# FFN 1's second matrix: hidden tiles 2 and 3 as a sixth half-size group of the seven-product scheme, and a new order of work around the transposes behind it

## The chip, the cores and the metric

The kernel runs on one core of a Trainium2 chip. The metric is the time of one execution on the device in microseconds; the number that counts is the median of several runs. The engines are TensorE (PE; PEld is its weight load), VectorE (DVE), ScalarE (ACT), GpSimd (POOL) and SyncE (SP, which here only starts transfers). POOL starts the transfers that add into SBUF.

## What is computed

One layer of a streaming encoder on 512 tokens of width 1024, all in float32: half-step FFN 1, a mixer (recurrent branch and attention) and half-step FFN 2, each between RMS norms. What matters here is FFN 1 and the entry of the mixer:

```python
f = swiglu(rms_norm(h, ffn1_pre_g), ffn1_w1, ffn1_w3, ffn1_w2)   # (silu(x @ w1) * (x @ w3)) @ w2, hidden width 2816
h = h + 0.5 * rms_norm(f, ffn1_post_g)
u = rms_norm(h, mix_pre_g)
... = u @ w_in                                                   # xr is its first part here
```

## The kernel before, in words

**Split numbers.** Every float32 operand of a matmul is split into a high part (a copy in a format that TensorE takes at full rate) and a low part (the difference). `split2` (L224) does it: ScalarE writes the copy (L226), VectorE the difference (L227). A product is then three matmuls: high x high, high x low, low x high.

**FFN 1's first matrices.** The hidden width has 22 tiles of 128. Tiles 0 to 3 (`NC1 = 4`) are computed one by one. Tiles 0 and 1 (`NG = 2`) go through silu at once; of tiles 2 and 3 the two products are copied to the buffers `kept`, and gate (`gate_kept`, L1357), silu (`silu_kept`, L1360) and product (`swiglu_kept`, L1363) come later, at hooks of the next stage (`KEPT_AT`). Tiles 4 to 21 come in pairs (`Pairs`, L844): each of 18 jobs makes one product of two tiles from seven smaller ones and prepares the weights of the next job meanwhile (`prep`). The dictionary `late` hangs further work on points (job, place) of these pairs.

**FFN 1's second matrix** (`w2a`; helpers `blocks` L759, `Halves` L601, `tok_gemm` L378). `GS_A` lists groups of hidden tiles: (4, 6) stands for tiles 4, 5, 6, 7, and there are five such groups, `G = 5`, 20 tiles. Each group's product with the matrix, cut in two halves of hidden tiles, tokens and columns, is made with seven products instead of eight. They are named, in the order of the work, m1, m5, m2, m6, m3, m7, m4 (L607). Product m of group i is **unit** number u = (place of m) x G + i; within a name the groups add into the same PSUM banks: m1, m6, m7 and m4 into `bu`, m5 and m3 into `bx`, m2 into `bc`, each a pair of banks for two token tiles. A unit of two tile pairs is 12 matmuls of 512 columns (`unit`, L716): 2 pairs, 2 token tiles, 3 matmuls. A group with one entry in its tuple has one pair of tiles and half of everything: 6 matmuls, operands of half width, high and low of the weights in one buffer.

Each unit needs operands, and `prep` (L686) makes them in unit order: one split of a weight tile, one split of a hidden tile, and the sums for later products (`sums`, L662). The second and further weight operands come by transfers that add into a negated copy (`T`, L647: ScalarE negates, POOL starts the transfer); `t1` and `s1` do the first of these ahead of time, from the pairs' points. `step(u)` (L749) prepares up to unit u + 4 (`LEAD = 5`), runs the **hooks** of u, issues the unit's matmuls and, behind the last group of m1, m5, m6 and m7, has the banks copied or added out (`out`, L732).

**Tiles 2 and 3** (`TAIL_A`) are no group. They are multiplied the plain way (`classical`, L426, through `mm_tok`, L249 to L257): 4 token tiles x 2 column halves x 2 hidden tiles x 3 matmuls of 512 columns. Their weights are loaded and split by `tails` (L421), their hidden tiles by `Hidden.to` (L590) into `hT`.

**From FFN 1 to the mixer** (`tok_gemm`, L434 to L482, and L501 to L555). With token tiles t = 0 to 3 the written order is: units of m1 to m3; plain products of t = 0 and 1; two more preps; the first of the mixer's weights `xr` split (`x_split`); norm(0); the units of m7; plain products of t = 2, 3 (one half); preps of m4; norm(1); the units of m4 for their first token tile, `step(u, (0,))`; transposes tr(0) of the normed tile of t = 0; a plain product; the first unit of m4 for its second token tile; tr(1); norm(2); the other units of m4; a last plain product; the mixer's first `xr` unit for tokens 0 to 255 (`start`, L504, 24 matmuls of 256 columns); tr(2); norm(3); two more such units; tr(3); a fourth; then tokens 256 to 511 of all four.

`norms` (L326) is two norms in a row (the FFN's post norm and the mixer's pre norm) on ScalarE and VectorE; it writes `hg`, half by VectorE (L345), half by ScalarE (L346), stores the new residual by SP (L342), and calls `mid` in its middle. Where a part of the sum was copied out before, the norm begins with an add (L308). `transpose_mm` (L349) turns `hg` on TensorE into `tr`, `transpose_out` (L359) splits it into `uT`, the operand of the mixer, and `transpose_xf` (L371) copies it for later sums.

Each engine does its instructions in the order in which the program writes them, and so does each queue of transfers (SP's, POOL's). Buffers come from one pool of 42 slots of 4 KB per partition and from 8 PSUM banks; an instruction that reuses one waits for the last reader. `MARKS_A` and `X_AT` give the steps at whose hooks the tail's loads, the residual's loads (`h_back`) and the `xr` loads are started. FFN 2's second matrix (`w2b`, `last_gemm`, L797) has six groups already, `GS_B`, the last of them `(20,)`, of half size, and no plain tiles; no mixer follows it.

Of the kernel before, what the change touches and what calls it, by code (L numbers as in the profile page):

```python
# [13 lines left out]
ALU = mybir.AluOpType  # L14
# [37 lines left out]
def hybrid_layer(ctx: ExitStack, tc: tile.TileContext, a: dict, out: bass.AP):  # L52
# [14 lines left out]
    def bank(name="ps"):  # L67
        uid[0] += 1
        return pp.tile([P, 512], F32, tag="ps", name=f"{name}_{uid[0]}")
# [308 lines left out]
    def tok_gemm(nm, xs, n, R, gpost_name, scale, gpre_name, first, x_to=None, xf=None, spill=False, then=None, eps=None, pre=None):  # L378
# [5 lines left out]
        acc = {}  # L384
# [36 lines left out]
        def tails():  # L421
            for i, k in enumerate(tail):
                x_to(F + i + 1)
                w[k] = get(nm, k, ahead=max(0, len(tail) - 1 - i), rawahead=0 if pre else 2)

        def classical(t, n_):  # L426
            for k in tail:
                new = k == tail[0] and (t > 1 and n_ == 1 if pre else k == 0)
                mm_tok(accs(t), xs[k], t, w[k], new, k == tail[-1], (n_,), bool(pre))

        def norm(t, mid=None):
            us[t] = norms(acc[t], t, g[0], scale, g[1], spill, ep(t), mid, pre and pre.part(t), (1, 0) if pre and t > 1 else (0, 1))

        if pre:  # L434
            G = pre.G
            pre.hooks[3 * G].append(vectors)
            pre.hooks[4 * G + 2].append(lambda: act.activation(small(1, "tiny"), veps[:, 0:1], AF.Abs_reciprocal_sqrt))
            pre.hooks[4 * G].append(lambda: act.activation(g[1], g[1], AF.Copy, scale=NEWT))
            x0 = st["get"] + len(tail)
            for i, u in enumerate(X_AT):  # L440
                pre.hooks[u].append(lambda i=i: dma_to(x0 + i + 1))

            def x_split(i, parts=(0, 1)):
                for p in parts:
                    dma_split(x0 + i, p)

            for u in range(5 * G):
                pre.step(u)
            tails()
            for t in range(2):  # L450
                acc[t] = [pre.bank["bc"][t], pre.bank["bx"][t]]
                for n_ in range(2):
                    classical(t, n_)
            pre.prep(5 * G + LEAD + 2)
            x_split(0)
            norm(0, lambda: x_split(1))
            pre.cap = 7 * G - 2
            for u in range(5 * G, 6 * G):
                pre.step(u)
            pre.cap = 7 * G  # L460
            for t in range(2, 4):
                acc[t] = [pre.bank["bu"][t - 2], bank("acc")]
                classical(t, 1)
            pre.prep(7 * G)
            pre.hid.eo.clear()
            x_split(2)
            norm(1, lambda: x_split(3, (0,)))
            for u in range(6 * G, 7 * G):
                pre.step(u, (0,))
            trs[0] = transpose_mm(us[0])  # L470
            transpose_out(trs[0], 0)
            classical(2, 0)
            pre.step(6 * G, (1,))
            trs[1] = transpose_mm(us[1])
            transpose_out(trs[1], 1)
            transpose_xf(trs[0], 0, xf)
            norm(2, lambda: [x_split(3, (1,)), transpose_xf(trs[1], 1, xf, (0,))])
            transpose_xf(trs[1], 1, xf, (1,))
            for u in range(6 * G + 1, 7 * G):
                pre.step(u, (1,))  # L480
            classical(3, 0)
            pre.bank.clear()  # L482
        else:
            tails()
            vectors()
            split_to(st["get"] + len(first))
            dma_to(st["split"] + 2)
            for t in range(NT):
                for n_ in range(2):
                    classical(t, n_)  # L490
                if t == NT - 1:
                    break
                if t >= 1:
                    trs[t - 1] = transpose_mm(us[t - 1])
                if t == NT - 2:
                    transpose_out(trs[t - 1], t - 1)
                norm(t)
                if t == 1:
                    transpose_out(trs[t - 1], t - 1, xf)
# [16 lines left out]
        k0, k1 = range(KT // 2), range(KT // 2, KT)  # L516
        if pre:
            start()
            trs[t - 1] = transpose_mm(us[t - 1])
            norm(t, between)  # L520
            transpose_out(trs[t - 1], t - 1, parts=(1,))
            start()
            start()
        else:
            start(range(3))
            trs[t - 1] = transpose_mm(us[t - 1])
            mm_feat(bs[0], ws[0], 0, 256, ks=range(3, KT))
            norm(t, between)
            transpose_out(trs[t - 1], t - 1, parts=(1,))
            transpose_xf(trs[t - 2], t - 2, xf, (1,))  # L530
            start()
            start(range(1))
# [5 lines left out]
            then()  # L538
        if not pre:
            mm_feat(bs[2], ws[2], 0, 256, ks=k0[1:])  # L540
        start()
        get_ahead()
        mm_feat(bs[0], ws[0], 256, 512)
        mm_feat(bs[1], ws[1], 256, 512)
# [214 lines left out]
    def blocks(nm, hid, pairs, late, h_src, gs, marks, in_slots, loads):  # L759
# [19 lines left out]
        if pairs.R is None:  # L779
            late[end - 4, 1] = [lambda i=i: half.s1(i) for i in range(4)]  # L780
            late[end - 3, 1] = [lambda: half.load(3)]
            late[end - 2, 1] = [lambda i=i: half.t1(i) for i in range(2)]
            late[end - 1, 2] = [lambda: half.prep(1, False)]
            late[end, 1] = [lambda: half.t1(2)]
        else:
            late[5, 1].append(lambda: half.s1(0))
            late[9, 1].append(lambda: half.s1(1))
            late[13, 1] = [lambda: half.s1(2)]
            for i in (1, 2, 3):
                late.setdefault((end, i), []).insert(0, lambda i=i: half.t1(i - 1))  # L790
            late[end, 1].append(lambda: half.s1(3))
            for i in (3, 4):
                hooks[i - 3].append(lambda i=i: half.t1(i))
        pairs.run(ahead, late)
        return half
# [566 lines left out]

    def swiglu_kept(f):  # L1363
        t = kept.pop(f)
        dve.tensor_tensor(out=t[:, 1, :], in0=t[:, 0, :], in1=t[:, 1, :], op=ALU.mult)
        hid.f[f] = t[:, 1, :]

    X1.update((b, uview(*q)) for b, q in (("b11", (0, 0)), ("b21", (1, 0)), ("b22", (1, 1))))
    P_ = pairs_a.prep
# [23 lines left out]
    late[4, 2], late[5, 2] = [softplus_exp], [softplus_ratio]  # L1393
    late[5, 3], late[6, 2] = [lambda: softplus_terms((13, 11, 9))], [lambda: softplus_terms((7, 5))]
    late[7, 2], late[8, 2] = [lambda: softplus_terms((3, 1))], [softplus_out]

    h.clear()
    half = blocks("w2a", hid, pairs_a, late, lambda t: a["x"][t * P : (t + 1) * P, :], GS_A, MARKS_A, 6 * len(GS_A), LOAD_A)
    X1 = pairs_a = late = None
    for fn, at_ in zip((gate_kept, silu_kept, swiglu_kept), KEPT_AT):  # L1400
        for f, u in zip(range(NG, NC1), at_):
            half.hooks[u].insert(0, lambda f=f, fn=fn: fn(f))
    xf = {(hh, th): slot([P, 4, 256], name="xf") for hh in range(2) for th in range(2)}
    bs = tok_gemm(
        "w2a", hid, FT, len(TAIL_A), "ffn1_post_g", 0.5, "mix_pre_g", [("xr", i) for i in range(4)], xf=xf, spill=True, eps=veps, pre=half)
# [446 lines left out]

BY_POOL = {("wg", i) for i in range(2, 8)} | {("wk", 0), ("wk", 1)}

TAIL_A = (2, 3)
KEPT_AT = (15, 16), (18, 19), (19, 20)
LEAD = 5
U_SLOTS = 4
LOAD_A, LOAD_B = (0, 3, 5, 5), (0, 4, 5, 6)
GS_A = (4, 6), (8, 10), (12, 14), (16, 18), (0, 20)  # L1860
MARKS_A = (17, 18), (21, 22), (23, 26, 28, 29)
X_AT = (22, 24, 26, 28)

TAIL_B = ()
GS_B = (0, 2), (4, 6), (8, 10), (12, 14), (16, 18), (20,)
# [6 lines left out]
NC1 = 4  # L1872
# [57 lines left out]
```

## Time and profile before

| | us |
|---|---|
| median of 3 runs | 1100.61 (1100.34 to 1101.22) |
| the profiled execution | 1100.36 |
| its span, first to last instruction | 1098.4 |
| TensorE busy, share of the span | 1089.5, 99% |
| VectorE busy | 930.2, 85% |
| ScalarE busy | 707.6, 64% |
| POOL busy | 418.0, 38% |

A row of a timeline has the start in us, the duration in us, the engine, the line of the kernel, the operation, what it writes and reads, the shape, and how many are merged; a bracket at its end is the idle time of the engine before it and what ended it. `whi` and `wlo` are the split weights, `hx` and `uT` the split hidden tiles of a unit. A row of groups has, behind the bar, busy time and mean duration in ns of one. A row of waits has engine, tile and line of who waited, for whom, the sum in us, how often, and the longest. A row of windows has the stretch, its length, busy time of PE, PEld, DVE, ACT and POOL with the number of instructions, TensorE's granted clock, the share of the DMA engines and GB/s. A matmul's duration is longer than the distance from one to the next, since they overlap.

### The profile page before, as it was taken

To read this page: it belongs to the slowest core of one execution; us is meant where nothing else is said; L and a number is where in the kernel's file an instruction comes from. 1 tells how busy PE (TensorE), PEld (TensorE's weight loads), DVE (VectorE), ACT (ScalarE), POOL (GpSimd) and SP (SyncE) were. 2 spreads that over 40 slices of the span, in tenths; PEclk is the share of its full clock that TensorE was granted. 3 is DMA by queue.
4 is the path that set the end of the run, shared out by engine and by line. 5 is a ranking of instruction groups with operands and counts; after the bars stand their busy time and mean duration, and the time that the engine had idled before them with its cause. 6 is when DMAs were issued, how large, how long until landed. Compare 5 with 4: busy or idle time off the path is not lost.

```text
span 1098.4 us, 18110 instructions
## 1 busy us (share of the span) xinstructions
PE 1089.5 (99%) x6856; PEld 986.2 (90%) x6856; DVE 930.2 (85%) x1334; ACT 707.6 (64%) x1230; POOL 418.0 (38%) x348
## 2 busy tenths in 40 slices
PE   9999999999999999999999999999999999999997
PEld 8899999998888878899888888888999999998886
DVE  5987999989988998887778867767889989889996
ACT  7756555598878778656656654446555455578872
POOL 0144933232002513242556573010877656633200
PEclk9999999999999999999999999999999999999999
DMA  9325663389767642156122335352323323449923
GB/s 340 120 83 143 131 150 115 105 187 231 218 171 228 178 122 77 39 173 249 58 95 79 114 136 211 137 188 85 129 78 115 108 86 108 147 101 239 213 75 134
DMA packets 53895, 156.46 MB, mean 142 GB/s; under 512 B 5536, under 2 KB 7456, under 8 KB 53808
## 3 DMA queue, kind: packets, MB, share of 16 engines
q1 hardware_dynamic: 40848, 124.59, 32.3%
q0 software_dynamic: 12672, 30.19, 14.8%
q8 instruction: 54, 0.88, 0.3%
q10 hardware_dynamic: 288, 0.52, 0.1%
q14 instruction: 33, 0.27, 0.1%
HBM read 139.57 MB, written 13.62 MB: 139 GB/s over the span
## 4 chain that ended last, share of the span: by engine, by line
PE 93%; DVE 3%; ACT 2%; DMA 1%; issue 1%; DVEq 0%; POOL 0%; ACTq 0%; POOLq 0%
PE c L838 13%; PE c L839 13%; PE c L840 13%; PE f L237 9%; PE f L238 9%; PE f L239 9%; PE hw L728 5%; PE hw L729 5%; PE hw L730 5%; PE acc L257 1%; PE acc L256 1%; PE acc L255 1%; PE pt L1692 1%; DMA raw_xr<-in_xr_dram 1%; DVE wlo L227 1%
## 5 line engine op out<-in xcount | busy, mean ns | idle before, releaser
L839 PE MATMUL c<-uT,wlo 128*128 128x256 f32 x516 | 146.0, 283 | 0.0
L840 PE MATMUL c<-uT,whi 128*128 128x256 f32 x516 | 146.0, 283 | 0.0
L838 PE MATMUL c<-uT,whi 128*128 128x256 f32 x516 | 146.0, 283 | 0.0
L838 PE MATMUL c<-Xh,whi 128*128 128x256 f32 x504 | 142.7, 283 | 0.0
L839 PE MATMUL c<-Xh,wlo 128*128 128x256 f32 x504 | 142.6, 283 | 0.0
L237 PE MATMUL f<-uT,whi 128*128 128x512 f32 (+1 forms) x380 | 138.6, 365 | 0.0
L238 PE MATMUL f<-uT,wlo 128*128 128x512 f32 (+1 forms) x380 | 136.9, 360 | 0.0
L239 PE MATMUL f<-uT,whi 128*128 128x512 f32 (+1 forms) x380 | 136.9, 360 | 0.0
L840 PE MATMUL c<-Xl,whi 128*128 128x256 f32 x456 | 129.0, 283 | 0.0
L227 DVE TENSOR_TENSOR wlo<-S,whi 128x1024 fp32r<-128x1024 f32 x86 | 121.0, 1407 | 5.9 <-POOL OL L1728 3.1
L226 ACT ACTIVATE whi<-S 128x1024 fp32r<-128x1024 f32 x86 | 88.5, 1054 | 29.1 <-DVE S L887 28.0
L839 PEld LDWEIGHTS c<-uT,wlo 128*128 128x128 f32 x516 | 99.0, 192 | 0.2
L838 PEld LDWEIGHTS c<-uT,whi 128*128 128x128 f32 x516 | 99.0, 192 | 0.2
L840 PEld LDWEIGHTS c<-uT,whi 128*128 128x128 f32 x516 | 99.0, 192 | 0.0
L838 PEld LDWEIGHTS c<-Xh,whi 128*128 128x128 f32 x504 | 96.8, 192 | 0.3 <-issue 0.3
L839 PEld LDWEIGHTS c<-Xh,wlo 128*128 128x128 f32 x504 | 96.8, 192 | 0.0
L728 PE MATMUL hw<-whi,uT 128*128 128x512 f32 x228 | 88.7, 389 | 0.0
L730 PE MATMUL hw<-whi,uT 128*128 128x512 f32 x228 | 88.7, 389 | 0.0
L840 PEld LDWEIGHTS c<-Xl,whi 128*128 128x128 f32 x456 | 87.5, 192 | 0.0
L729 PE MATMUL hw<-wlo,uT 128*128 128x512 f32 x216 | 84.0, 389 | 0.0
L237 PEld LDWEIGHTS f<-uT,whi 128*128 128x128 f32 x380 | 71.7, 189 | 12.1 <-issue 1.7
L239 PEld LDWEIGHTS f<-uT,whi 128*128 128x128 f32 x380 | 71.7, 189 | 10.9
(435 smaller groups left out, 3209.8 us busy)
## 6 DMA issues: line engine op xcount, KB each, us to landing
raw_w1b<-in_w1b_dram SPq DMA_DIRECT2D x22, 512.0 KB, 4.2
raw_w3b<-in_w3b_dram SPq DMA_DIRECT2D x22, 512.0 KB, 4.4
raw_w3a<-in_w3a_dram SPq DMA_DIRECT2D x21, 512.0 KB, 5.0
raw_w1a<-in_w1a_dram SPq DMA_DIRECT2D x20, 512.0 KB, 4.4
raw_w2a<-in_w2a_dram SPq DMA_DIRECT2D x17, 512.0 KB, 5.4
raw_wg<-in_wg_dram SPq DMA_DIRECT2D x16, 512.0 KB, 3.5
raw_w2a<-in_w2a_dram POOLq DMA_DIRECT2D x15, 512.0 KB, 9.4
raw_w2b<-in_w2b_dram SPq DMA_DIRECT2D x15, 512.0 KB, 6.3
```

What stands on the lines that cost most here:

```text
L226: act.activation(hi, src, AF.Copy)
L227: dve.tensor_tensor(out=lo, in0=src, in1=f32(hi), op=ALU.subtract)
L237: pe.matmul(ps[:, c0:c1], wh[:, s], h_, start=k == 0 and c0 == 0, stop=False, skip_group_check=True)
L238: pe.matmul(ps[:, c0:c1], wl[:, s], h_, start=False, stop=False, skip_group_check=True)
L239: pe.matmul(ps[:, c0:c1], wh[:, s], l_, start=False, stop=k == KT - 1, skip_group_check=True)
L255: pe.matmul(acc[n], x[:, 0, c], wh[:, s], start=first, stop=False, skip_group_check=skip)
L728: pe.matmul(ps, xs[:, 0, j, c], hi[:, j, :], start=start and j == 0, stop=False, skip_group_check=True)
L729: pe.matmul(ps, xs[:, 0, j, c], lo[:, j, :], start=False, stop=False, skip_group_check=True)
L730: pe.matmul(ps, xs[:, 1, j, c], hi[:, j, :], start=False, stop=i == self.G - 1, skip_group_check=True)
L838: pe.matmul(ps, wh[:, s], xh, start=first, stop=False, skip_group_check=True)
L839: pe.matmul(ps, wl[:, s], xh, start=False, stop=False, skip_group_check=True)
L840: pe.matmul(ps, wh[:, s], xl, start=False, stop=k == 3, skip_group_check=True)
```

## The change

Tiles 2 and 3 become a sixth group `(2,)` of half size, so `G` is 6 and there are 42 units, u0 to u41, with the half-size ones at u5, u11, u17, u23, u29, u35 and u41. `TAIL_A` is empty; the plain products, their loads and their splits are gone. Gate, silu and product of tiles 2 and 3 move from hooks of this stage to jobs 1 and 2 of the pairs, and the product is written to the group's buffer. The early negations (`t1`) start one place earlier. The preps are cut anew around norm(0), the last two units of m7 are run one token tile after the other, and two units of m4 instead of one stand between tr(0) and tr(1). Behind it the mixer's second `xr` unit is cut in two halves of 12 matmuls, one ahead of tr(2), one behind it, and the fourth likewise around tr(3). The hooks' step numbers are moved to suit.

```diff
             for u in range(5 * G):
                 pre.step(u)
-            tails()
             for t in range(2):
                 acc[t] = [pre.bank["bc"][t], pre.bank["bx"][t]]
-                for n_ in range(2):
-                    classical(t, n_)
-            pre.prep(5 * G + LEAD + 2)
+            pre.prep(5 * G + LEAD + 3)
             x_split(0)
             norm(0, lambda: x_split(1))
-            pre.cap = 7 * G - 2
-            for u in range(5 * G, 6 * G):
+            pre.prep(7 * G - 2)
+            for u in range(5 * G, 6 * G - 2):
                 pre.step(u)
-            pre.cap = 7 * G
+            for t in range(2):
+                for u in range(6 * G - 2, 6 * G):
+                    pre.step(u, (t,))
+                if t == 0:
+                    pre.prep(7 * G)
             for t in range(2, 4):
-                acc[t] = [pre.bank["bu"][t - 2], bank("acc")]
-                classical(t, 1)
-            pre.prep(7 * G)
+                acc[t] = [pre.bank["bu"][t - 2], None]
             pre.hid.eo.clear()
             x_split(2)
             norm(1, lambda: x_split(3, (0,)))
...
             trs[0] = transpose_mm(us[0])
             transpose_out(trs[0], 0)
-            classical(2, 0)
-            pre.step(6 * G, (1,))
+            for u in range(6 * G, 6 * G + 2):
+                pre.step(u, (1,))
             trs[1] = transpose_mm(us[1])
             transpose_out(trs[1], 1)
-            transpose_xf(trs[0], 0, xf)
-            norm(2, lambda: [x_split(3, (1,)), transpose_xf(trs[1], 1, xf, (0,))])
+            x_split(3, (1,))
+            norm(2, lambda: [transpose_xf(trs[0], 0, xf), transpose_xf(trs[1], 1, xf, (0,))])
             transpose_xf(trs[1], 1, xf, (1,))
-            for u in range(6 * G + 1, 7 * G):
+            for u in range(6 * G + 2, 7 * G):
                 pre.step(u, (1,))
-            classical(3, 0)
...
         if pre:
             start()
+            start(k0)
             trs[t - 1] = transpose_mm(us[t - 1])
             norm(t, between)
             transpose_out(trs[t - 1], t - 1, parts=(1,))
+            mm_feat(bs[1], ws[1], 0, 256, ks=k1)
             start()
-            start()
+            start(k0)
...
-        start()
+            start()
+        else:
+            mm_feat(bs[3], ws[3], 0, 256, ks=k1)
...
+            late[11, 2] = [lambda: half.s1(5)]
             late[13, 1] = [lambda: half.s1(2)]
-            for i in (1, 2, 3):
-                late.setdefault((end, i), []).insert(0, lambda i=i: half.t1(i - 1))
+            for at_, i in (((end - 1, 3), 0), ((end, 1), 1), ((end, 2), 2)):
+                late.setdefault(at_, []).insert(0, lambda i=i: half.t1(i))
             late[end, 1].append(lambda: half.s1(3))
-            for i in (3, 4):
+            for i in (3, 4, 5):
                 hooks[i - 3].append(lambda i=i: half.t1(i))
...
-        dve.tensor_tensor(out=t[:, 1, :], in0=t[:, 0, :], in1=t[:, 1, :], op=ALU.mult)
-        hid.f[f] = t[:, 1, :]
+        hid.f[f] = hid.place(f)
+        dve.tensor_tensor(out=hid.f[f], in0=t[:, 0, :], in1=t[:, 1, :], op=ALU.mult)
...
+    for at_, fn in zip(((1, 2), (2, 1), (2, 2)), (gate_kept, silu_kept, swiglu_kept)):
+        late[at_] = [lambda f=f, fn=fn: fn(f) for f in range(NG, NC1)]
...
-    for fn, at_ in zip((gate_kept, silu_kept, swiglu_kept), KEPT_AT):
-        for f, u in zip(range(NG, NC1), at_):
-            half.hooks[u].insert(0, lambda f=f, fn=fn: fn(f))
...
-TAIL_A = (2, 3)
-KEPT_AT = (15, 16), (18, 19), (19, 20)
+TAIL_A = ()
...
-GS_A = (4, 6), (8, 10), (12, 14), (16, 18), (0, 20)
-MARKS_A = (17, 18), (21, 22), (23, 26, 28, 29)
-X_AT = (22, 24, 26, 28)
+GS_A = (4, 6), (8, 10), (12, 14), (16, 18), (0, 20), (2,)
+MARKS_A = (), (), (27, 31, 33, 34)
+X_AT = (26, 28, 31, 33)
```

## The prediction

> **What bounds the kernel now.** I read the page's first lines, then the view of waits for TensorE alone, then the timeline of TensorE over the stage that the change touches.
>
> ```profile
> span 1098.4 us, 18110 instructions
> PE 1089.5 (99%) x6856; PEld 986.2 (90%) x6856; DVE 930.2 (85%) x1334; ACT 707.6 (64%) x1230; POOL 418.0 (38%) x348
> PE tr L355 <- DVE hg L345: 0.8, 2, 0.6
> ```
>
> TensorE is the bound of the whole kernel: after its start it waits for data only twice, 0.8 us together, both times where a transpose (L355) needs a normed tile `hg`. So the time changes by what TensorE has less to do, and by what its waits become. The stage in question, in TensorE's own rows:
>
> ```profile
> 231.94 0.40 PE L728 MATMUL hw<-whi,hx 128*128 128x512 f32 x1
> 299.97 0.39 PE L255 MATMUL hw<-whi,hT 128*128 128x512 f32 x1
> ...
> 328.54 0.27 PE L355 MATMUL tr<-ident,hg 128*128 128x128 f32 x1
> ...
> 331.92 0.39 PE L730 MATMUL hw<-whi,hx 128*128 128x512 f32 x1
> 332.86 0.33 PE L355 MATMUL tr<-ident,hg 128*128 128x128 f32 x1 [0.55 <-DVE hg L345]
> ...
> 349.90 0.28 PE L238 MATMUL f<-uT,wlo 128*128 128x256 f32 x1
> 350.02 0.28 PE L239 MATMUL f<-uT,whi 128*128 128x256 f32 x1
> 350.51 0.30 PE L355 MATMUL tr<-ident,hg 128*128 128x128 f32 x1 [0.20 <-DVE hg L345]
> ```
>
> From 231.94 to 299.97 stand 25 units of 12 matmuls, 300: 0.227 us from one start to the next (the 0.39 is how long one is in flight). A matmul of 256 columns takes 0.12 (349.90 to 350.02). Of the transposes, tr(0) at 328.54 goes straight on. tr(1) comes 0.94 after the matmul before it, 0.71 more than a pitch; tr(3) 0.49, 0.37 more. These 1.08 us are all that better cover could win.
>
> **The change part by part.** *Matmuls.* The classical tiles go:
>
> ```profile
> L255 PE MATMUL hw<-whi,hT 128*128 128x512 f32 x12 | 4.8, 396 | 0.0
> L255 PE MATMUL acc<-whi,hT 128*128 128x512 f32 x4 | 1.6, 389 | 0.0
> ```
>
> 16 on each of the three lines L255 to L257, so 48 matmuls. The half-size group brings 7 units of 6, 42. Gain 6 x 0.227 = 1.36 us. The mixer's 256-column matmuls stay the same in number; 12 of them move from behind tr(3) to before it.
>
> Where TensorE would be without waits: units u0 to u29 (five names of five full units and one of half size) are 330 matmuls and end at 231.94 + 74.9 = 306.8. The 66 of m7 and the first token half of m4, 33, bring tr(0) to 329.2 (before: 328.54). Eight transposes and 12 matmuls stand between tr(0) and tr(1) in both, 3.6 us (328.54 to 331.92 and a pitch), so at 332.8 it wants tr(1), and with it hg(1).
>
> *When hg(1) is there.* VectorE and ScalarE prepare units, then norm(0), then units, then norm(1), each in program order. The point from which both can be timed is the copy-out of m6 (`out`, L742), where ScalarE waits for TensorE. FFN 2 already runs with six groups, the last of half size, so its rows give that point and the price of a half unit:
>
> ```profile
> 986.49 0.40 PE L728 MATMUL hw<-whi,hx 128*128 128x512 f32 x1
> 1045.88 1.28 ACT L742 ACTIVATE hc<-hw 128x512 f32<-128x512 f32 x2 [3.30 <-PE hw L730]
> 1047.05 1.05 ACT L226 ACTIVATE whi<-raw_w2b 128x1024 fp32r<-128x1024 f32 x1
> 1048.52 0.62 ACT L226 ACTIVATE whi<-raw_w2b 128x512 fp32r<-128x512 f32 x1
> 1049.35 1.05 ACT L226 ACTIVATE whi<-raw_w2b 128x1024 fp32r<-128x1024 f32 x1
> 1049.88 0.68 DVE L227 TENSOR_TENSOR whi<-raw_w2b,whi 128x512 fp32r<-128x512 f32 x1
> 1050.82 1.22 DVE L227 TENSOR_TENSOR wlo<-raw_w2b,whi 128x1024 fp32r<-128x1024 f32 x1
> ```
>
> ScalarE is free of the copy-out 60.56 us after the stage's first matmul (986.49 to 1047.05): here at 231.94 + 60.56 = 292.5. A half unit costs ScalarE 0.83 (1048.52 to 1049.35) and VectorE 0.94 (1049.88 to 1050.82). A full one, and the things that FFN 1 has besides:
>
> ```profile
> 290.34 1.06 ACT L438 ACTIVATE bc_mix_pre_g<-bc_mix_pre_g 128x1024 f32<-128x1024 f32 x1 [1.22 <-DMA bc_mix_pre_g<-in_mix_pre_g_dram]
> 297.29 1.28 ACT L437 ACT_TABLE_LOAD   x1
> 298.70 1.05 ACT L226 ACTIVATE whi<-raw_w2a 128x1024 fp32r<-128x1024 f32 x1
> 299.65 0.61 ACT L226 ACTIVATE uT<-hEO 128x512 fp32r<-128x512 f32 x1
> 300.17 1.05 ACT L226 ACTIVATE whi<-raw_w2a 128x1024 fp32r<-128x1024 f32 x1
> 299.78 1.23 DVE L227 TENSOR_TENSOR wlo<-raw_w2a,whi 128x1024 fp32r<-128x1024 f32 x1 [0.35 <-ACT whi L226]
> 301.52 1.22 DVE L227 TENSOR_TENSOR wlo<-raw_w2a,whi 128x1024 fp32r<-128x1024 f32 x1
> 308.47 0.69 DVE L308 TENSOR_TENSOR hc<-hw,hc 128x512 f32<-128x512 f32 x1
> ```
>
> A full unit: ScalarE 1.47 (298.70 to 300.17; 0.95 of it the weights), VectorE 1.74. The table load takes 1.41 (297.29 to 298.70), the scaling L438 0.95 like any 1024-wide copy. From 292.5 ScalarE does u28 1.47, the scaling 0.95 (hook 24), u29 0.83, u30 1.47, the table 1.41 (hook 26) and the weights of u31 0.95, to 299.6. VectorE then has u31 to u37 ahead of norm(0), six full and one half: 6 x 1.74 + 0.94 = 11.4, so norm(0) starts at 311.0, where it started at 308.47: **2.5 us later**, though its accumulators are complete at 306.8. `prep(5 * G + LEAD + 3)` puts four units behind step 29's own ahead of the norm; before it was three.
>
> From norm(0) to norm(1):
>
> ```profile
> 323.81 1.06 ACT L169 ACTIVATE whi<-raw_xr 128x1024 fp32r<-128x1024 f32 x1 [2.68 <-DMA raw_xr<-in_xr_dram]
> 325.72 0.62 ACT L310 ACTIVATE junk<-hc 128x512 f32<-128x512 f32 x1
> 324.12 0.69 DVE L308 TENSOR_TENSOR hc<-hw,hc 128x512 f32<-128x512 f32 x1
> 332.05 0.75 DVE L345 SCALAR_TENSOR_TENSOR hg<-h,r,bc_mix_pre_g 128x512 f32<-128x512 f32 x1
> ```
>
> VectorE: 15.65 before (three full units, m7's two adds), now a half unit more: 311.0 + 16.6 = 327.6, with the add 328.2. ScalarE: the raw tile of `xr` 2 is loaded on SP's queue behind norm(0)'s store (L342), which is not moved past it, and came 15.34 after norm(0)'s start; its split 1.91; so 328.2 again. Norm(1)'s first square was at 325.72: 2.5 late by both ways. hg(1), 332.80 before, comes at 335.3: tr(1) at 335.35 instead of 332.86, after a wait of 2.6. Behind it in TensorE's queue stands all the rest; ScalarE's and VectorE's copies of tr(1) wait for it, and behind them norm(2), so the whole chain moves.
>
> *Behind tr(1).* Norm(2) and norm(3) lose the L308 add; what that frees is the idle time that ended on it:
>
> ```profile
> 336.41 0.63 ACT L310 ACTIVATE junk<-hc 128x512 f32<-128x512 f32 x1 [0.71 <-DVE hc L308]
> 343.69 0.63 ACT L310 ACTIVATE junk<-hc 128x512 f32<-128x512 f32 x1 [0.18 <-DVE hc L308]
> 351.80 1.29 DVE L367 TENSOR_TENSOR uT<-tr,uT 128x512 fp32r<-128x512 f32 x2 [0.24 <-ACT uT L365]
> ```
>
> The chain tr(1) to tr(3) took 17.65 and takes 0.89 less, 16.76 (the split of `xr` 3 and the xf copies of tr(0) change places on ScalarE, about 1 us each); TensorE's own work there, 17.28 without its wait, loses 9 matmuls (2.04) and gains 12 short ones (1.44): 16.68. So tr(3) at 352.1, 1.6 later than 350.51, and the 12 short ones behind it are gone: 1.6 - 1.44 = **+0.2 us**. By TensorE's account: -1.36 - 1.08 + 2.6 + 0.1, the same. The halves ahead of tr(2) and tr(3) cover nothing that is missing, as the norms, not the transposes, are late. Behind tr(3) TensorE reaches the new uT columns 2.5 us after tr(3)'s start instead of 3.9; their first low half is ready 1.9 after it (351.80 and half of 1.29). If that cover fails, up to 1.4 us more.
>
> *Costed at nothing.* Gate, silu and product of tiles 2 and 3 go to pairs 1 and 2:
>
> ```profile
> 62.86 2.04 DVE L227 TENSOR_TENSOR wlo<-raw_w1a,whi 128x1024 fp32r<-128x1024 f32 x1 [1.57 <-ACT whi L226]
> ```
>
> two VectorE operations of L308's size (0.69) in each. In pair 1 an idle stretch of 1.57 takes them; where none is left, VectorE is 1.4 us late with weights that it prepares a whole pair ahead of their use. The added unit preparations of m1 to m6 move VectorE and TensorE alike (0.94 and the small sums against 6 x 0.227 = 1.36 each); FFN 2's six groups show no TensorE wait in the view of waits. SP's queue loses the two loads of the tail tiles and gets three of half that size; POOL gets three accumulating loads of half size, and its load of `bc_mix_pre_g` goes behind a later unit; that one ended a wait before (L438's bracket). If it is later than 294.0, ScalarE is late by as much: nothing, up to the 1.2 us of that bracket. Step 34 now runs in two halves, so its hook loads x's last rows twice, behind the loads that matter: nothing. Four `f` banks of PSUM stand ahead of tr(3) where three did, but the two `acc` banks of tiles 2 and 3 are gone: nothing, and if a bank is late, some of norm(3)'s 0.7 us operations.
>
> **Rivals.** *The norm is not late* (1098.2): if VectorE gets to norm(0) by 308.4, both waits go and -1.36 - 1.08 = -2.4 is left. For it: FFN 2's stage has no wait; against: its transposes don't exist, and the sum above misses by 2.5.
>
> *The clock falls in the new wait* (1103.5, the slower side). The granted clock at the end of the kernel:
>
> ```profile
> 1091.03 0.39 PE L730 MATMUL hw<-whi,hx 128*128 128x512 f32 x1
> 1094.00:1095.00 1.00, 0.00 (x0) 0.00 (x0) 1.00 (x3) 0.00 (x0) 0.00 (x0) 0.72 0.00 0
> 1095.00:1096.00 1.00, 0.00 (x0) 0.00 (x0) 0.19 (x1) 0.00 (x0) 0.00 (x0) 0.50 0.74 282
> 1.09 4.21 PE L1148 MATMUL w<-warm 128*128 128x256 f32 x18 [1.09 <-POOL warm L1145]
> ```
>
> The last matmul ends at 1091.42, the clock goes to 0.50 at about 1094.44: 3.0 us of idleness. TensorE would be idle 2.4 us ahead of tr(1); 0.6 us more and it is there. Price: 0.6, and half rate for about as long as at the start, where 18 short matmuls took 4.21 (0.234 each), so 2.1: +0.2 + 0.6 + 2.1 = +2.9. [...]
>
> *Constants or raw tiles land late* (1102): bc_mix_pre_g or xr 2 behind more loads, 1 to 2 us on the same chain.
>
> **How the numbers follow.** The profiled execution took 1100.36, its span 1098.4 and 1.96 around it; +0.2 gives 1100.5. The median of the runs is 1100.61, so I predict 1100.8. Chances: this 0.57 (own range 1099.7 to 1102.3), norm in time 0.18, clock 0.15, late landing 0.10. 0.2% is 2.2 us, about what a measurement of this kernel can tell from no change: faster is below 1098.4, most of the first rival, 0.14; slower above 1102.8, the clock and some of the late cases, 0.22; within 0.64. The range 1098.2 to 1103.2 leaves out most of the clock case.
>
> **What would show it.** Right: 42 matmuls on L728 to L730 for the 48; norm(0)'s first L308 near 311; a wait ahead of tr(1) of some 2.6 for `hg`, almost none ahead of tr(3). Wrong: norm(0) at 308 or before; a wait at tr(2); a granted clock under 1.00 after tr(1); TensorE waiting for `whi` or `uT` inside the units.

## The result and the profile after

The changed kernel takes 1102.87 us (median of 19 runs), the kernel before 1100.84 in runs on the same chips: a ratio of 1.0017 [1.001, 1.0023], 1.9 us slower. The profiled execution took 1103.10, its span 1100.9. The forecast of 1100.8 missed by 2.1 us; the time is near that of the slower rival, whose price was 1103.5. It lies inside the range that was given, 1098.2 to 1103.2, and outside the 1099.7 to 1102.3 of the main account.

The head of the page of the changed kernel, then the view of waits for TensorE:

```profile
span 1100.9 us, 18128 instructions
...
PE 1089.4 (99%) x6850; PEld 986.1 (90%) x6850; DVE 937.1 (85%) x1347; ACT 711.2 (65%) x1243; POOL 423.8 (38%) x351
```

```profile
PE hw L730 <- ACT hx L226: 2.9, 1, 2.9
```

After the start of the kernel, the two waits for `hg` at the transposes are gone. In their place stands one, of 2.9 us, and it is ahead of a matmul of a unit. The timeline of TensorE shows which one:

```profile
321.78 0.39 PE L732 MATMUL hw<-whi,uT 128*128 128x512 f32 x1
325.07 0.47 PE L730 MATMUL hw<-whi,hx 128*128 128x512 f32 x1 [2.90 <-ACT hx L226]
...
326.40 0.63 PE L731 MATMUL hw<-wlo,hx 128*128 128x512 f32 x1
...
329.49 0.39 PE L730 MATMUL hw<-whi,hx 128*128 128x512 f32 x1
...
334.26 1.03 PE L355 MATMUL tr<-ident,hg 128*128 128x128 f32 x8
337.87 1.03 PE L355 MATMUL tr<-ident,hg 128*128 128x128 f32 x8
347.83 1.04 PE L355 MATMUL tr<-ident,hg 128*128 128x128 f32 x8
```

321.78 is the last matmul of m7 (it reads `uT`), 325.07 the first of m4 (it reads `hx`): 3.29 from start to start, 3.06 more than a pitch. And the matmuls behind it are slow: 325.07 to 329.49 are twelve pitches, 4.42 us where twelve of 0.227, the pitch in `before` at a granted clock of 1.00, make 2.72. That is 1.70 more. The windows of the same kernel tell why; TensorE's granted clock is the third column from the end:

```profile
325.00:326.00 1.00, 0.93 (x4) 0.78 (x5) 1.00 (x2) 0.00 (x1) 0.00 (x0) 0.84 0.96 352
326.00:327.00 1.00, 1.00 (x4) 0.81 (x3) 1.00 (x3) 0.45 (x1) 0.00 (x0) 0.50 1.05 430
...
329.00:330.00 1.00, 1.00 (x6) 0.83 (x5) 0.87 (x3) 0.61 (x2) 0.71 (x1) 0.96 1.00 397
```

Half rate began in the 326th microsecond, when TensorE had started again, and ended 3.4 us later. Now VectorE in the same stretch:

```profile
311.46 0.68 DVE L308 TENSOR_TENSOR hc<-hw,hc 128x512 f32<-128x512 f32 x1
...
320.75 1.23 DVE L227 TENSOR_TENSOR wlo<-raw_w2a,whi 128x1024 fp32r<-128x1024 f32 x1 [1.01 <-ACT whi L226]
...
323.63 0.69 DVE L227 TENSOR_TENSOR hx<-hEO,hx 128x512 fp32r<-128x512 f32 x1
324.24 0.69 DVE L742 TENSOR_TENSOR hc<-hw,hc 128x512 f32<-128x512 f32 x1
...
328.11 0.68 DVE L308 TENSOR_TENSOR hc<-hw,hc 128x512 f32<-128x512 f32 x1
...
335.23 0.75 DVE L345 SCALAR_TENSOR_TENSOR hg<-h,r,bc_mix_pre_g 128x512 f32<-128x512 f32 x1
```

Norm(0) starts at 311.46. Behind it come the preps of u38 and u39 and then, from 324.24 to 324.93, the add that copies m7's first token tile out of its bank (`out`, L742). m4 accumulates into the same banks `bu`, so its first matmul may not write before that add has read; it starts 0.14 after the add's end. The view of waits names ScalarE's `hx` instead, since the last event ahead of 325.07 was the end of this operation at 325.00:

```profile
324.60 0.40 ACT L226 ACTIVATE hx<-hEO 128x256 fp32r<-128x256 f32 x1
...
328.88 0.63 ACT L310 ACTIVATE junk<-hc 128x512 f32<-128x512 f32 x1 [0.32 <-DVE hc L308]
```

The first row is u41's operand, 128x256; u36, whose matmul waited, has had its own since 309.8 (the second row is norm(1)'s first square). The two candidates are 0.07 us apart, and only a run can tell them apart.

In the kernel before, the twelve plain matmuls stood between m7 and m4. Its TensorE rows and VectorE's two adds:

```profile
318.79 0.39 PE L730 MATMUL hw<-whi,uT 128*128 128x512 f32 x1
...
321.73 0.39 PE L728 MATMUL hw<-whi,hx 128*128 128x512 f32 x1
```

```profile
L740 DVE TENSOR_TENSOR hc<-hw,hc x2: 681/682/683, 319.4 to 320.0; 128x512 f32<-128x512 f32 x2
```

m7's last matmul started at 318.79, its adds were over by 320.7, m4 began at 321.73: the plain products covered the adds, and were removed.

The sum of the profiled executions: -1.36 (six matmuls), -1.08 (the waits at tr(1) and tr(3)), +3.06 (the wait), +1.70 (half rate), +0.28 (the stage's first matmul comes at 232.22 instead of 231.94, from the first 20 us of the execution, where nothing was changed) = +2.6. The spans differ by 2.5.

Other executions of the changed kernel bear the last big term out. 3.4 us at half rate take 0.0015 off the mean granted clock of such a span. Two executions have a mean clock of 0.998, where those of the kernel before have 0.998 or 0.999, and took 1101.03 and 1101.48 us; fifteen have 0.996 or 0.997 and took 1102.42 to 1103.10. (The other two are one with 0.995, 1104.08 us, and one in a slow state, 1182.20 us with 0.85.) So without the half rate the loss would be 0.2 to 0.6 us, where -1.36 - 1.08 + 3.06 gives 0.6, and the half rate adds 1.4 to 1.8.

### The profile page after: what moved, and what is told of

Same layout as the page of the kernel before. It is cut to its first block, busy times and chain, and to the rows that moved or that the text cites. A ratio compares the mean times of both kernels' runs of the same rounds, so it can differ in the third digit from the quotient of the medians.

```text
span 1100.9 us, 18128 instructions
## 1 busy us (share of the span) xinstructions
PE 1089.4 (99%) x6850; PEld 986.1 (90%) x6850; DVE 937.1 (85%) x1347; ACT 711.2 (65%) x1243; POOL 423.8 (38%) x351
## 4 chain that ended last, share of the span: by engine, by line
PE 70%; ACT 1%; DVE 1%; DMA 0%; issue 0%; DVEq 0%; ACTq 0%
PE f L237 9%; PE f L239 9%; PE f L238 9%; PE c L843 8%; PE c L842 8%; PE c L841 8%; PE hw L730 4%; PE hw L732 4%; PE hw L731 4%; PE acc L257 1%; PE acc L255 1%; PE acc L256 1%; PE pt L1694 1%; PE s L1658 1%; PE s L1657 1%; PE tr L355 1%
## 5 line engine op out<-in xcount | busy, mean ns | idle before, releaser
L227 DVE TENSOR_TENSOR wlo<-S,whi 128x1024 fp32r<-128x1024 f32 x86 | 116.7, 1357 | 6.4 <-ACT whi L226 3.2
L730 PE MATMUL hw<-whi,uT 128*128 128x512 f32 x240 | 93.4, 389 | 0.0
L732 PE MATMUL hw<-whi,uT 128*128 128x512 f32 x240 | 93.4, 389 | 0.0
L731 PE MATMUL hw<-wlo,uT 128*128 128x512 f32 x216 | 84.0, 389 | 0.0
```

Of the source, the lines that this page charges most:

```text
L227: dve.tensor_tensor(out=lo, in0=src, in1=f32(hi), op=ALU.subtract)
L730: pe.matmul(ps, xs[:, 0, j, c], hi[:, j, :], start=start and j == 0, stop=False, skip_group_check=True)
L731: pe.matmul(ps, xs[:, 0, j, c], lo[:, j, :], start=False, stop=False, skip_group_check=True)
L732: pe.matmul(ps, xs[:, 1, j, c], hi[:, j, :], start=False, stop=i == self.G - 1, skip_group_check=True)
```

## The experiments

Each kernel was timed with the kernel before on the same chip; the ratio and, in brackets, its 95% interval are against that. Differences between two runs below are of medians, in part from different chips; where they are 1.2 us or less, the intervals of the ratios overlap.

**1. The add ahead of two preps** (e1_add_first; changed kernel):

```diff
-            pre.prep(7 * G - 2)
+            pre.cap = 7 * G - 4
...
                 if t == 0:
+                    pre.cap = 7 * G
                     pre.prep(7 * G)
```

> Edit: the preps of u38 and u39 stand behind VectorE's add of m7's first token tile (L742), no longer ahead of it. Theory 1 (the first matmul of m4 adds into the bank that this add has to read first, and the add stood behind the two preps, until 324.93): the wait of 2.9 at m4's first unit goes; the add takes the idle 1.01 us of VectorE behind norm(0), so norm(1) comes 0.6 earlier and hg(1) at about 335.3; TensorE wants tr(1) at 333.1, so a wait of about 2.2 for hg stands there, where the prediction had it. About 1100.6 us if the clock holds in it, 1102.2 if it falls again. Theory 2 (the wait is for what the view of waits names, ScalarE's hx, an operand): the operands of u36 and u37 are made when they were, those of u38 to u41 no earlier, so the wait of 2.9 stays where it is, 1102.9 us.

1106.07 us, ratio 1.0045 [1.0033, 1.0058]. The wait at m4's first unit is gone, and a larger one stands at tr(1), as the timelines of TensorE and VectorE show:

```profile
338.01 1.97 PE L355 MATMUL tr<-ident,hg 128*128 128x128 f32 x8 [4.87 <-DVE hg L345]
```

```profile
320.05 0.69 DVE L743 TENSOR_TENSOR hc<-hw,hc 128x512 f32<-128x512 f32 x1 [0.41 <-PE hw L733]
...
331.02 0.69 DVE L311 SCALAR_TENSOR_TENSOR fg<-hc,bc_ffn_post_g 128x512 f32<-128x512 f32 x1 [2.93 <-DMA h<-in_x_dram]
```

The add (L743 here) ran at 320.05, and m4 followed m7 without a pause. So Theory 1 holds for the cause of the wait, though ScalarE's work was where it had been. The time went the wrong way for a reason that neither theory had: VectorE's write into norm(1)'s buffer `fg` waited 2.93 us for a load of x. The clock fell in the wait as well: the eight transposes took 1.97 us instead of 1.03, and by the windows TensorE ran at half rate from 336.08 to 342.92.

**2. The same, with x's last rows loaded once** (e6_add_one_load), and **3. the single load alone** (e5_one_load):

```diff
-            for fn in self.hooks.get(u, ()):
+            for fn in self.hooks.get(u, ()) if ts[0] == 0 else ():
```

> Edit: the add of m7's first token tile ahead of the preps of u38 and u39, as in the run e1_add_first, and the last rows of x loaded once. In e1_add_first the wait at m4's first unit was gone, but VectorE waited 2.93 us in norm(1) for a load of x into a buffer. Theory 1 (that buffer was the one of the load that nobody uses): the wait of 2.93 goes, hg(1) comes near 335.3, tr(1) waits about 2.2 us, 1100.6 us with a clock of 1.00 in it, 1102.2 if the clock falls. Rival (it is the load that the norm needs, or another): VectorE waits as in e1_add_first, 1106 us.

> Edit: a step that is run in two token halves runs its hooks only with the first half, so that the last rows of x are loaded once and not twice. If the prediction's zero for this step holds in the changed kernel (no engine waits there for a load of x): 1102.9 us, the same wait of 2.9 at m4's first unit. If the second load's buffer and its 0.5 MB hold something up that shows only as a late norm(1) (ScalarE waits 1.55 us ahead of x_split(2)): up to 1 us less.

The two together took 1103.43 us (1.0024 [1.0015, 1.0033]). VectorE's wait of 2.93 for the load is gone, so the buffer was that of the second load, which nobody uses. The rest of the expectation was 1 to 3 us too low. The view of waits, and ScalarE's row behind it:

```profile
PE tr L355 <- DVE hg L345: 3.2, 1, 3.2
```

```profile
327.13 1.06 ACT L169 ACTIVATE whi<-raw_xr 128x1024 fp32r<-128x1024 f32 x1 [2.43 <-DMA raw_xr<-in_xr_dram]
```

With VectorE early, ScalarE waits for `xr` 2, whose load is queued behind norm(0)'s store, so hg(1) is no earlier than in the changed kernel, TensorE waits 3.2 us at tr(1), where the prediction had 2.6, and the clock falls there. The single load alone took 1103.51 us (1.0024 [1.0015, 1.0033]) with the same wait of 2.9: no gain, as priced. Its profiled execution, 1104.37 us, ran at half rate for twice as long (below); two others of its eleven, with a mean clock of 0.998, took 1101.40 and 1101.61.

**4. Six extra matmuls in the wait** (e2_fill6; changed kernel):

```diff
+            wh, _, wx = pre.ops[6 * G - 2]
...
+            fill = bank("fill")
+            for k in range(6):
+                pe.matmul(fill, wx[:, 0, 0, :P], wh[:, 0, :], start=k == 0, stop=k == 5)
```

> Edit: six extra matmuls of 512 columns, whose result nobody reads, between the last matmul of m7 and the first of m4. They take 6 x 0.227 = 1.36 us of the 2.9 us in which TensorE waited and release nothing. Theory 1 (the wait ends with VectorE's add, whatever TensorE does, and the idle time then halves the clock for 3.45 us): m4 starts at 325.07 as before, the idle time left is 1.5 us, the clock stays at 1.00, and the 1.6 us of half-rate matmuls go: about 1101.3 us. Rival (the clock falls for another reason than the idle time, or half rate costs nothing that counts): 1102.9 us, or 1104.3 if the six matmuls come on top.

1101.70 us (1.001 [1.0001, 1.0018]), 1.2 below the changed kernel by the medians and 0.8 by the ratios, with more work:

```profile
322.24 1.52 PE L465 MATMUL fill<-whi,uT 128*128 128x512 f32 x6
325.32 0.47 PE L734 MATMUL hw<-whi,hx 128*128 128x512 f32 x1 [1.56 <-ACT hx L226]
325.63 0.39 PE L735 MATMUL hw<-wlo,hx 128*128 128x512 f32 x1
```

m4 starts 0.25 later than in the changed kernel, as m7 ends 0.23 later there (its last matmul at 322.01 for 321.78): the six matmuls moved nothing. The idle time is 1.56, and the matmuls behind it follow at 0.23. The granted clock is 1.00 from 321 to 345. So the half-rate stretch came from the idle time. It cost 1.70 us in the changed kernel's profiled execution; the median of this run points the same way, as do the executions of the changed kernel with a mean clock of 0.998.

**5. Two low parts on GpSimd** (e3_low_on_pool; changed kernel), and **6. the same with the add ahead of three of the four preps** (e4_pool_and_add):

```diff
+                if self.nm == "w2a" and u in (36, 37):
+                    act.activation(hi, src, AF.Copy)
+                    pool.tensor_tensor(out=lo, in0=src, in1=f32(hi), op=ALU.subtract)
+                else:
+                    split2(hi, lo, src)
```

> Edit: the low parts of the weights of u36 and u37 (two operations of 1.22 us ahead of norm(0)) are made by GpSimd, no longer by VectorE. Theory 1 (VectorE's queue is late by that much work, through norm(0), the add, norm(1)): norm(0) starts 2.4 earlier, near 309.0, the add ends near 322.5, so the wait at m4's first unit is about 0.5, the clock stays at 1.00, hg(1) comes near 333.4 and tr(1) waits 0 to 0.3: about 1098.7 us. Theory 2 (ScalarE's operands): ScalarE's work is the same, so 1102.9 us or little less. If GpSimd slows VectorE while it works, up to 2 us of the gain go.

> Edit: the two low parts on GpSimd, and of the four preps behind norm(0) only u38's stands ahead of the add of m7's first token tile. Theory 1: no wait at m4's first unit, VectorE reaches norm(1) near 325.7, hg(1) near 333, TensorE wants tr(1) at 333.1, so no wait is left and the clock holds: about 1098.2 us, 4.8 below the changed kernel and 2.5 below the kernel before. Theory 2: 1102.9 us.

1105.61 us (1.0039 [1.0027, 1.0052]) and 1102.95 us (1.0016 [1.0007, 1.0025]); in both Theory 1's time was missed, by 6.9 and 4.8 us. GpSimd's row and VectorE's of the first:

```profile
306.94 6.90 POOL L711 TENSOR_TENSOR wlo<-raw_w2a,whi 128x1024 fp32r<-128x1024 f32 x2 [24.73 <-ACT whi L710]
```

```profile
308.07 3.51 DVE L227 TENSOR_TENSOR hx<-hEO,hx 128x512 fp32r<-128x512 f32 x2
311.50 0.68 DVE L308 TENSOR_TENSOR hc<-hw,hc 128x512 f32<-128x512 f32 x1
312.27 2.12 DVE L311 SCALAR_TENSOR_TENSOR fg<-hc,bc_ffn_post_g 128x512 f32<-128x512 f32 x1
```

GpSimd took 3.45 us for each. Two operations of VectorE that take 1.29 together took 3.51 beside them, and one of 0.69 took 2.12: 3.65 us lost for the 2.4 saved. Not every operation beside them was slow: that of 311.50 took its usual 0.68. Why the others were slow is not shown. Norm(0) came no earlier (311.50), TensorE's wait at m4's first unit grew to 4.2 us, and the clock fell behind it, to 0.50. The view of waits of the second names the add itself, now that no event of ScalarE lies between, and no longer an operand:

```profile
PE hw L735 <- DVE hc L747: 2.4, 1, 2.4
PE tr L355 <- DVE hg L345: 1.3, 1, 1.3
```

**7. ScalarE's two extra operations moved** (e7_scalar_moved; changed kernel, x loaded once), and **8. the same with the add ahead of three of the four preps** (e8_all):

```diff
-            pre.hooks[4 * G + 2].append(lambda: act.activation(small(1, "tiny"), ...
+            pre.hooks[4 * G - 3].append(lambda: act.activation(small(1, "tiny"), ...
-            pre.hooks[4 * G].append(lambda: act.activation(g[1], g[1], AF.Copy, scale=NEWT))
...
             pre.prep(5 * G + LEAD + 3)
+            act.activation(g[1], g[1], AF.Copy, scale=NEWT)
```

> Edit: x loaded once; ScalarE's table load moves from behind u30 to a place ahead of m6's copy-out, where ScalarE has been waiting (1.14 us ahead of u26), and the scaling of bc_mix_pre_g (L438) from behind u28 to behind u37's prep, where it waits 1.58 us. VectorE stays as it is. Theory (VectorE is late because ScalarE is, between 292 and 300: VectorE waited 0.66, 0.16, 0.23 and 1.16 us there for its copies): norm(0) starts 1.8 earlier, near 309.7, the add of m7 ends near 323.1, the wait at m4's first unit is 1.1 and the clock holds, hg(1) comes near 334.2 and tr(1) waits up to 0.6: about 1099.3 us. Rival (VectorE's own work sets it, ScalarE only seems to): norm(0) stays at 311.4 and the time at 1102.9.

> Edit: x loaded once, ScalarE's two operations moved as in e7_scalar_moved, and of the preps behind norm(0) only u38's ahead of the add of m7's first token tile. Theory: no wait at m4's first unit, norm(1) 2.4 earlier than in the changed kernel, hg(1) near 333.5 where TensorE wants tr(1) at 333.1; all but 0.5 of the 4.85 us go: about 1098.7 us, 2 below the kernel before. Rival: as for e7_scalar_moved, 1101 to 1103.

1100.26 us (0.9994 [0.9985, 1.0002]) and 1100.39 us (0.9995 [0.9986, 1.0004]): 2.6 and 2.5 below the changed kernel, not clear of the kernel before. Of the first, ScalarE's row, VectorE's, and the view of waits:

```profile
286.58 1.28 ACT L437 ACT_TABLE_LOAD   x1
```

```profile
298.32 1.23 DVE L227 TENSOR_TENSOR wlo<-raw_w2a,whi 128x1024 fp32r<-128x1024 f32 x1 [0.23 <-ACT whi L226]
...
309.92 0.68 DVE L308 TENSOR_TENSOR hc<-hw,hc 128x512 f32<-128x512 f32 x1
```

```profile
PE hw L730 <- ACT hx L226: 1.6, 1, 1.6
```

Norm(0) starts at 309.92, 1.5 earlier, of which 0.28 is the stage's own earlier start (231.94 for 232.22); the wait is 1.6, and the clock holds. So ScalarE's 1.41 and 0.95 us in front of u31 were a good part of why VectorE was late. In the second the wait is 1.4 us and stands at tr(1): taken from one place, it is at the next.

**9. The third second-half unit of m4 ahead of tr(1)** (e9_third_unit; on 8, with the load of `xr` 2 one place earlier):

```diff
-            for u in range(6 * G, 6 * G + 2):
+            for u in range(6 * G, 6 * G + 3):
...
-X_AT = (26, 28, 31, 33)
+X_AT = (26, 28, 30, 33)
```

> Edit: as e8_all, and the third unit of m4 for its second token half (u38, 6 matmuls, 1.36 us) stands ahead of tr(1), with the load of xr 2 one place earlier on SP's queue, ahead of that of x's rows for norm(1). In e8_all 1.4 us of wait for hg were left at tr(1). Theory 1 (the work is in the wrong place: cover moved ahead of tr(1) is cover gained): the wait at tr(1) falls to 0.1, 1099.0 us or a little more. Theory 2 (the chain of norms is the bound, tr(2) being due 9.2 after tr(1) by VectorE where TensorE has 10.0 of work): 8.6 of work are left behind tr(1), so 0.6 come back as a wait at tr(2) and some at tr(3): 1099.8 us.

1099.72 us (0.9991 [0.9983, 1.0]), the fastest version of the changed kernel, though by less than the intervals tell apart from run 8; the profiled execution, 1100.34, was the slowest of its eleven. The wait at tr(1) is gone, 0.6 stand at tr(2) and 0.2 at tr(3), as Theory 2 had it:

```profile
PE tr L355 <- DVE hg L345: 0.8, 2, 0.6
```

```profile
344.40 1.09 PE L355 MATMUL tr<-ident,hg 128*128 128x128 f32 x8 [0.58 <-DVE hg L345]
```

**10. The mixer's halves undone** (e11_halves_undone; on 7):

```diff
             start()
-            start(k0)
             trs[t - 1] = transpose_mm(us[t - 1])
...
-            mm_feat(bs[1], ws[1], 0, 256, ks=k1)
             start()
-            start(k0)
+            start()
...
-            mm_feat(bs[3], ws[3], 0, 256, ks=k1)
+            start()
```

> Edit: as e7_scalar_moved (1100.26 us), but the mixer's second and fourth unit whole and in the order of the kernel before: one unit ahead of tr(2), two ahead of tr(3), one behind it. The prediction counted the 12 short matmuls (1.44 us) as moved, not won, and said that the halves cover nothing that is missing. Theory 1 (in e7_scalar_moved TensorE reaches tr(2) and tr(3) just when hg is there): without the halves it waits up to 0.7 at tr(2) and 1.4 in all, and the 1.44 us of work stand behind tr(3): 1101.0 to 1101.7 us. Theory 2 (TensorE is late there anyway): no wait, 1100.3 us.

1101.18 us (1.0002 [0.9993, 1.0011]), 0.9 above 7. TensorE waits at tr(2) and tr(3):

```profile
344.08 1.09 PE L355 MATMUL tr<-ident,hg 128*128 128x128 f32 x8 [0.59 <-DVE hg L345]
...
351.16 1.06 PE L355 MATMUL tr<-ident,hg 128*128 128x128 f32 x8 [0.24 <-DVE hg L345]
```

This is Theory 1: the halves cover these waits. In run 7 TensorE reaches tr(2) 0.70 us and tr(3) 0.32 us after hg is there, less than the 1.44 us of the twelve short matmuls. In the changed kernel it is much the same, as VectorE's rows show:

```profile
346.33 0.75 DVE L345 SCALAR_TENSOR_TENSOR hg<-h,r,bc_mix_pre_g 128x512 f32<-128x512 f32 x1
...
353.32 0.75 DVE L345 SCALAR_TENSOR_TENSOR hg<-h,r,bc_mix_pre_g 128x512 f32<-128x512 f32 x1
```

hg is there at 347.08 and 354.07, tr(2) starts at 347.83 and tr(3) at 354.45, 0.75 and 0.38 later. So there, too, TensorE would wait without the halves; by these rows they are worth about 1 us (an estimate, no run undid them in the changed kernel itself).

**11 and 12. The kernel before, with ScalarE's operations moved**: both (e10_before_scalar, the table load's line as in 7), then the scaling alone (e12_before_scale_only).

```diff
-            pre.hooks[4 * G].append(lambda: act.activation(g[1], g[1], AF.Copy, scale=NEWT))
...
             pre.prep(5 * G + LEAD + 2)
+            act.activation(g[1], g[1], AF.Copy, scale=NEWT)
```

> Edit to the kernel before, not to the changed one: ScalarE's table load ahead of m6's copy-out, the scaling of bc_mix_pre_g behind the last prep ahead of norm(0), as in e7_scalar_moved. What the sixth group is worth with ScalarE out of the way in both is then e7_scalar_moved against this run. VectorE's waits between 290 and 300 were 0.52 and 0.35 there, so norm(0) may start up to 0.87 earlier. Theory 1 (the two waits of 1.08 us at tr(1) and tr(3) hang on that chain): up to 0.9 of them go, 1099.9 us. Theory 2 (they hang on the loads behind norm(0)'s store on SP's queue, which move with norm(0) too, or on TensorE's order): 1100.4 to 1100.8.

> Edit to the kernel before: only the scaling of bc_mix_pre_g moves, from its hook in the fourth name to behind the last prep ahead of norm(0). In e10_before_scalar the table load was moved too, but silu of the kept tiles still stood behind it and evicted the table: ScalarE loaded a table three times, the last of them inside norm(0) at 311.70. Here the table load stays. Theory 1 (VectorE ahead of norm(0) is late by ScalarE also in the kernel before: it waited 0.52 and 0.35 us there): norm(0) up to 0.5 earlier, 1100.3 us. Theory 2 (VectorE's own work, with the plain tiles' splits, fills that stretch): norm(0) within 0.2 of 308.5 and 1100.9 us, so that the same move which takes 2.6 us off the changed kernel is worth nothing in the kernel before.

With both, 1101.83 us (1.0008 [0.9999, 1.0017]): a miss of the edit, not an answer. The silu of the kept tiles stands behind the early table load in that kernel, and the tables were loaded twice more, the last time inside norm(0):

```profile
283.95 1.28 ACT L1361 ACT_TABLE_LOAD   x1
...
311.70 1.28 ACT L272 ACT_TABLE_LOAD   x1
```

With the scaling alone, 1099.92 us (0.9988 [0.9979, 0.9997]): below the 1100.3 of Theory 1. Norm(0) starts 0.4 earlier than in the kernel before, and 1.05 earlier if both are counted from the stage's first matmul (232.59 here, 231.94 there), so VectorE ahead of norm(0) hung on ScalarE in the kernel before too:

```profile
308.07 0.68 DVE L308 TENSOR_TENSOR hc<-hw,hc 128x512 f32<-128x512 f32 x1
```

Its view of waits for TensorE has only two rows, both of the start of the kernel, so the 1.08 us at tr(1) and tr(3) are gone:

```profile
PE w L1148 <- POOL warm L1145: 1.1, 1, 1.1
PE f L1198 <- ACT uT L1191: 0.2, 1, 0.2
```

So the kernel before, with one line moved, is as fast as the best version of the sixth group: 1099.92 beside 1099.72, with ratios of 0.9988 and 0.9991 to the kernel before.

## Why the prediction was right, and where it was wrong

**Right.** Six matmuls less: the half-size group's 7 x 2 matmuls that read their low part from `whi` on L731 are there in the view of groups, 14 where 7 units of 6 make 42 on three lines:

```profile
L731 PE MATMUL hw<-whi,uT 128*128 128x512 f32 x12 | 4.7, 389 | 0.0
L731 PE MATMUL hw<-whi,hx 128*128 128x512 f32 x2 | 0.8, 389 | 0.0
```

Norm(0) was forecast at 311.0 and came at 311.46; the stage itself came 0.28 later than before. Norm(1)'s first square was forecast at 328.2 and hg(1) at 335.3; they came at 328.88 and 335.98. So the mechanism, half a unit more on VectorE and ScalarE's chain ahead of it, held to 0.4 us, counted from the stage's own start. That the wait is of the size forecast as well (2.6 forecast, 2.9 to 3.1 measured) is partly luck: it is another wait, which ends with another operation. The costs set at nothing (kept operations, added preps, `bc_mix_pre_g`, banks, the second load) show no wait of TensorE in the changed kernel; in run 1, with another order of work, the second load cost VectorE 2.93 us.

**Wrong: where the wait is.** The step that failed is the sum that took TensorE from u29 through "the 66 of m7 and the first token half of m4, 33" to tr(0) at 329.2 without a wait. It counted m7's two adds as VectorE's time, and asked only what waits for `hg`. m4 writes the banks that the adds read, and the adds stand behind norm(0) and two preps; the 12 plain matmuls that had covered them were in the list of what goes, with their time alone. tr(0) came at 334.26, and tr(1) at 337.87, 1.9 after hg(1): VectorE's lateness was paid in full before tr(1). Run 2 put the wait where the prediction had it, at tr(1), and there it cost no less.

**Wrong: the clock.** That 2.4 us of idleness would keep it was an estimate, from the one distance of 3.0 at the end of the kernel before. The clock fell, as in the rival with 0.15, but in a wait that this rival did not name, ahead of m4 and not ahead of tr(1). Its price was 0.6 more of wait and 2.1 of half rate; measured were 0.5 and 1.7. (The half rate of the start, from which the 2.1 came, is read from its short matmuls, 0.234 us each where others of 256 columns take 0.12; the granted clock in its windows is 1.00.) Its condition was set too high: the wait of 2.9 us was enough, and in run 3 the clock fell 2.06 us after the last matmul's end. That the time still lies in the range given is luck as far as the main account goes, which had neither the place of the wait nor the half rate.

**The rival that the norm is not late** (1098.2) needs more than ScalarE's help: runs 7 to 9 made norm(0) 1.3 us earlier, counted from the stage's first matmul, and the best of them still waits 0.8 us for the chain of norms, at 1099.72.

**Wrong: the halves.** The prediction said that the halves ahead of tr(2) and tr(3) "cover nothing that is missing". Its own sum says otherwise: it has 16.68 us of TensorE's work beside 16.76 of the chain of norms, so without the 1.44 of the short matmuls ahead of them TensorE would have waited at tr(2) or tr(3). Run 10 gives the halves 0.9 us, and the rows of the changed kernel about as much.

What stays open is the exact condition of the clock's fall, whether run 9's gain on run 8 (0.7 us by the medians, 0.4 by the ratios) is real, and how much of it is the third unit's and how much the earlier load's.

## What to carry to other kernels

When work is removed, ask what it stood in front of: list each instruction that follows it on its engine with all that this waits for, the reads of the bank that it will write among them. A chain that is late moves its wait from place to place when the order is changed (m4's first unit, tr(1), tr(2)) and it shrinks when the engine that sets it gets work out of its way, here by moving ScalarE's two operations to where ScalarE had been waiting (2.9 us to 1.6 in run 7). And try the cheap fix on the old kernel too: moving one line gave it as much as the new group had at its best.

## What the runs showed of the hardware

**In this stage the clock fell for 3.4 us, or for twice as long.** From the window means the ends of each half-rate stretch can be worked out: a mean of 0.84 over one microsecond is 0.32 us at half rate. In the changed kernel that gives 325.68 to 329.08, 3.40 us. Run 3, then run 2:

```profile
324.00:325.00 1.00, 0.09 (x1) 0.12 (x1) 1.00 (x3) 0.84 (x3) 0.00 (x0) 0.53 1.05 299
...
330.00:331.00 1.00, 1.00 (x4) 0.77 (x4) 0.96 (x2) 0.68 (x2) 0.00 (x0) 0.56 0.83 111
```

```profile
335.00:336.00 1.00, 0.00 (x0) 0.00 (x0) 0.93 (x3) 0.64 (x2) 0.00 (x0) 0.77 0.83 340
...
338.00:339.00 1.00, 1.00 (x4) 0.80 (x4) 0.84 (x2) 0.83 (x2) 0.00 (x0) 0.53 0.00 0
```

Run 3: 324.06 to 330.88, 6.82 us, twice 3.41. Run 2: 335.54 to 338.94, 3.40. Run 1's windows give 6.84. How long TensorE was idle did not settle alone whether the clock fell. In the changed kernel it fell after 2.90 us of idle time, when TensorE had been at work again for 0.6; in run 3 it fell 2.06 us after the last matmul's end (322.00), 0.85 before the next one began (324.91). Yet 2.4 us of idle time in run 6's profiled execution and 1.56 in run 4's left the clock at 1.00. So the price of one wait differs from execution to execution: nothing in those of the changed kernel and of run 3 with a mean clock of 0.998, 1.7 us in the changed kernel's profiled one, and about 3.0 in run 3's, where matmuls ran for 5.97 of the 6.82 us (an estimate, half of the 5.97). What decides it is not shown: no run moved the wait alone.

**A load that nobody reads stopped an engine** through the buffer that it still occupied: 2.93 us of VectorE in run 1, and no wait of TensorE in the changed kernel. Runs 1 and 2 differ in that load alone; that the order of work decides who gets the buffer is the reading of it, not a measurement.
